# Low parts of the split weights 32 bytes off the other tiles, and the products of gate and up grouped by high and low

## The chip, the cores and the metric

The kernel runs on one core of a Trainium2 chip. The metric is the device time of one execution in microseconds, as the median of several runs. The names of the engines in the rows are PE (TensorE, the matmuls), PEld (its weight loads, which run beside the matmuls), DVE (VectorE), ACT (ScalarE), POOL (GpSimd) and SP (SyncE, which issues most of the DMAs).

## The reference

Two layers of a decoder trunk on 256 tokens of width 1024, all in float32. Each layer is a half-step SwiGLU network, a mixer of three kinds of attention heads with one input and one output projection, and a second SwiGLU network. The change touches the SwiGLU networks and the tiles in which all weights are split:

```python
def swiglu(h, w_gate, w_up, w_down):
    return (jax.nn.silu(h @ w_gate) * (h @ w_up)) @ w_down

for l in range(DEPTH):                                   # 2
    x = x + 0.5 * swiglu(rmsnorm(x, ffn1_norm[l]), ffn1_w_gate[l], ffn1_w_up[l], ffn1_w_down[l])
    h = rmsnorm(x, mix_norm[l])
    ...
    x = x + o @ w_out[l]
    x = x + 0.5 * swiglu(rmsnorm(x, ffn2_norm[l]), ffn2_w_gate[l], ffn2_w_up[l], ffn2_w_down[l])
return rmsnorm(x, final_norm)
```

w_gate and w_up are 1024 x 2816, w_down is 2816 x 1024.

## The kernel before

Every product of two float32 matrices is made of three products of a shorter format, fp32r: each operand is split into a high part (a copy rounded to fp32r) and a low part (what is left), and high x high, high x low and low x high are summed in PSUM. For a weight tile `raw` that has come by DMA, `split` (L91) makes the high part `wh` on ACT (L96) and the low part `wl` on DVE (L97). `split_tiles` (L77) takes both from rings of five buffers of 4096 bytes per partition. In the built program every one of these buffers, and every other tile of that size, begins at a multiple of 512 bytes within its partition. The normed input of a network is `xhl` (L180): for each of eight blocks k of 128 rows the 256 columns of the high part, then the 256 of the low part.

A network (`ffn`, L243) goes through 22 blocks f of 128 columns of gate and up. For f = 1 to 21 each of gate (bank `pg`, tag g0) and up (bank `pu`, tag g1) takes eight wide products, `wh` against high and low part of the input side by side (512 columns), and eight narrow ones, `wl` against the high part alone (256 columns); the list `steps` (L294 to L297) sets their order, and the loop at L299 issues them at L308. For f = 0 the list is another one (L282 to L292), of 256-column products alone. Behind the products of block f stand the twelve 512-column matmuls of `down` for block f - 1 (L251, by `mm3` and `mm` at L89): h hi x wh, h hi x wl in the rows' names `wl,hh`, and h lo x wh.

Between them lies the chain that makes h from the two banks: the second half of gate's bank copied out (ACT, L324), added to the first (DVE, L325), times the norm's row (L326), Silu (ACT, L327); the second half of up's bank copied (ACT, L330), added (DVE, L331), multiplied with the gate (L333), and h split (ACT `hh` L336, DVE `hl` L337). After the last block `take` (L263) adds the four sums into x_tok, and `norm_in` (L195) transposes it for what comes next. The mixer's projections use the same `wh` and `wl`.

The program's text is written stage by stage; the order in which each engine gets its instructions is set by a scheduler that builds the queues of all engines from the program, so a change in one engine's list can move instructions on the others. Each engine then runs its queue in order and waits on semaphores. All weight loads go over SP's queue in order, and a load waits for its `raw` buffer (ring of four) to be free.

At the start ACT's queue loads the small tables `norm_rows` (L119) and `pos_rows` (L137), which `late_columns` (L166) transposes on PE in block f = 1 of the first network; `compressed` in the mixer loads its `w2` (L647, L648).

A few tiles of before do not begin at a multiple of 512 bytes: `maskc`, which is streamed through PE in the mixer, begins 32 bytes off a multiple of 64 and 480 off one of 512, and `pcm`, which is loaded as the stationary operand of a transpose, 32 bytes off a multiple of 64 and 352 off one of 512. Neither is fp32r: `maskc` is bf16, `pcm` float32.

Of the kernel before, what the change touches and what calls it, by code (L numbers as in the profile page):

```python
# [10 lines left out]
F32 = mybir.dt.float32  # L11
# [8 lines left out]
T = 256  # L20
# [3 lines left out]
KD = D // 128  # L24
# [38 lines left out]
def trunk(ctx, tc, a, out):  # L63
# [4 lines left out]
    sb = ctx.enter_context(tc.tile_pool(name="sb", bufs=1))  # L68
    con = ctx.enter_context(tc.tile_pool(name="con", bufs=1))
    small = ctx.enter_context(tc.tile_pool(name="small", bufs=1))  # L70
    big.tile([128, 96], F32, name="pad")
    ps = ctx.enter_context(tc.tile_pool(name="ps", bufs=2, space=PSUM))

    def raw_tile():
        return sb.tile([128, 2048], F32, name="raw", tag="raw", bufs=4)

    def split_tiles(n):  # L77
        h = sb.tile([128, 1024], F32R, name="wh", tag="wh", bufs=5)
        lo = sb.tile([128, 1024], F32R, name="wl", tag="wl", bufs=5)
        return h[:, :n], lo[:, :n]  # L80

    def bank(tag):
        return ps.tile([128, 512], F32, name="bk" + tag, tag=tag, bufs=2)
# [32 lines left out]
    x_tok = big.tile([128, 2, D], F32, name="x_tok")  # L116
    for t in range(2):
        nc.sync.dma_start(x_tok[:, t], a["x"][0, t * 128:(t + 1) * 128, :])
    norm_rows = con.tile([64, 128], F32, name="norm_rows")  # L119
    r0 = 0  # L120
    gcol = {}
    first_rows = con.tile([16, 128], F32, name="first_rows")
# [11 lines left out]
    cosn, sinn = tab[:, :, 0:16], tab[:, :, 16:32]  # L134
    cosm, sinm = tab[:, :, 32:64], tab[:, :, 64:96]
    cmask, cvalid = tab[:, :, 96:111], tab[:, :, 111:112]
    pos_rows = con.tile([64, 128], F32, name="pos_rows")  # L137
    for i, n in enumerate(("nsa_cmp_pos_k", "nsa_cmp_pos_v")):
        nc.scalar.dma_start(pos_rows[32 * i:32 * i + 32], a[n].rearrange("l (j q) d -> (l j) (q d)", q=2))
    gbias = con.tile([128, DEPTH, 18], F32, name="gbias")  # L140
# [39 lines left out]
    xhl = big.tile([128, KD, 2, T], F32R, name="xhl")  # L180
    xh, xl = xhl[:, :, 0], xhl[:, :, 1]
    oh = big.tile([128, KD, T], F32R, name="oh")
    ol = big.tile([128, KD, T], F32R, name="ol")

    state = {}

    def late_loads():
        if state.pop("late", None):
# [44 lines left out]
    def mm3(o, w, mov, first, last):  # L233
        mm(o, w[0], mov[0], first, False)
        mm(o, w[0], mov[1], False, False)
        mm(o, w[1], mov[0], False, last)

    def load_unit(w, c, n):
        t = raw_tile().rearrange("p (k f) -> p k f", k=KD)[:, :, :n]
        nc.sync.dma_start(t, w[:, c:c + n].rearrange("(k p) f -> p k f", p=128))  # L240
        return t

    def ffn(pre, l, nxt=None, final=False, first=False):  # L243


        wg, wu, wd = a[pre + "_w_gate"][l], a[pre + "_w_up"][l], a[pre + "_w_down"][l]
        rb = None
        acc = {}
        hs, ds = {}, {}

        def down(f, t, c):  # L251
            h, lo = hs[f]
            w = (ds[f][0][:, c * 512:c * 512 + 512], ds[f][1][:, c * 512:c * 512 + 512])
            s = slice(t * 128, t * 128 + 128)
            mm3(acc[t, c], (h[:, s], lo[:, s]), w, f == 0, f == NF - 1)

        tokens_first = [(t, c) for t in range(2) for c in range(2)]
        columns_first = [(t, c) for c in range(2) for t in range(2)]
        order = tokens_first if final else columns_first

        def take(t, c):
            x = x_tok[:, t, c * 512:c * 512 + 512]
            DVE.scalar_tensor_tensor(x, acc[t, c], r05[:, t:t + 1], x, op0=OP.mult, op1=OP.add)  # L263

        for f in range(NF):
            o = 0
            if f % 2 == 0 or first and f == 1:
                n = 128 if first and f < 2 else 256
                if not (first and f == 0):
                    rg, ru = [load_unit(w, f * 128, n) for w in (wg, wu)]  # L270
            else:
                o = 128
            if f % 2 == 0:
                rd = raw_tile().rearrange("p (j f) -> p j f", j=2)
                nc.sync.dma_start(rd, wd[f * 128:f * 128 + 256, :].rearrange("(j p) f -> p j f", p=128))
            if first and f == 0:
                G, U = W0
            else:
                G = split(rg[:, :, o:o + 128], 1024, "p (k f) -> p k f", k=KD)
                U = split(ru[:, :, o:o + 128], 1024, "p (k f) -> p k f", k=KD)  # L280
            pg, pu = bank("g0"), bank("g1")
            if f == 0:  # L282
                if first:
                    groups = [(o, w, (k,)) for o, w in ((pg, G), (pu, U)) for k in (0, 2, 4, 6, 1, 3, 5, 7)]
                else:
                    groups = [(o, w, ks) for ks in ((0, 1, 2, 3), (4, 5, 6, 7)) for o, w in ((pg, G), (pu, U))]
                steps = []
                for o, w, ks in groups:
                    hi = [(o[:, :T], w[0], xh, k) for k in ks]
                    mid = [(o[:, :T], w[1], xh, k) for k in ks]  # L290
                    lo = [(o[:, T:], w[0], xl, k) for k in ks]
                    steps += hi + lo + mid if first else hi + mid + lo  # L292
            else:
                steps = []  # L294
                for o, w in ((pg, G), (pu, U)):
                    steps += [(o, w[0], xhl.rearrange("p k i q -> p k (i q)"), k) for k in range(KD)]
                    steps += [(o[:, :T], w[1], xh, k) for k in range(KD)]  # L297
            seen = {id(pg): 0, id(pu): 0}
            for j, (o, w, m, k) in enumerate(steps):  # L299
                b = id(pg) if o.tensor is pg.tensor else id(pu)  # L300
                last = not any(s[0].tensor is o.tensor for s in steps[j + 1:])
                args = (o, w[:, k], m[:, k])
                flags = dict(start=seen[b] == 0, stop=last, skip_group_check=True)
                seen[b] = 1
                if first and f == 0:
                    then("pe", PE.matmul, *args, **flags)
                else:
                    PE.matmul(*args, **flags)  # L308
            if f == 1:
                if state.get("late"):  # L310
                    late_columns()
                for i, (t, c) in enumerate(order):
                    acc[t, c] = bank("a%d" % (i // 2))
            if f > 0:
                for t, c in order if f < NF - 1 else order[:2]:
                    down(f - 1, t, c)
            if rb is None:
                r = rstd_col()
                r05 = small.tile([128, 2], F32, name="r05", tag="r05", bufs=2)
                DVE.tensor_scalar(r05, r, 0.5, None, op0=OP.mult)  # L320
                rb = rstd_rows(r)
            gn = tmp(0)[:, :T]
            g2 = tmp(3)[:, :T]
            ACT.copy(g2, pg[:, T:])  # L324
            DVE.tensor_tensor(gn, pg[:, :T], g2, op=OP.add)  # L325
            DVE.tensor_tensor(gn, gn, rb, op=OP.mult)  # L326
            ACT.activation(gn, gn, AF.Silu)  # L327
            un = tmp(1)[:, :T]
            u2 = tmp(3)[:, :T]
            ACT.copy(u2, pu[:, T:])  # L330
            DVE.tensor_tensor(un, pu[:, :T], u2, op=OP.add)  # L331
            h = tmp(2)[:, :T]
            DVE.tensor_tensor(h, gn, un, op=OP.mult)  # L333
            hh = sb.tile([128, T], F32R, name="hh", tag="hh", bufs=2)
            hl = sb.tile([128, T], F32R, name="hl", tag="hl", bufs=2)
            ACT.activation(hh, h, AF.Copy)  # L336
            DVE.tensor_tensor(hl, h, hh.bitcast(F32), op=OP.subtract)  # L337
            hs[f] = (hh, hl)
            ds[f] = split(rd[:, f % 2], 1024)
            if final and f == 2:  # L340
                state["fnorm"] = sb.tile([128, D], F32, name="fnorm", tag="pj")
                nc.sync.dma_start(state["fnorm"], a["final_norm"].partition_broadcast(128))
            if f == 3:
                late_loads()

        if final:
            for t in range(2):
                if t == 1:
                    for c in range(2):
                        down(NF - 2, t, c)  # L350
                sm = small.tile([128, 2], F32, name="fs", tag="fs", bufs=2)
                zs = []
                for c in range(2):
                    down(NF - 1, t, c)
                    take(t, c)
                    zs.append(finish(t, c, sm))
                store(t, zs, sm)
        else:
            for t in range(2):
                down(NF - 1, t, 0)  # L360
                take(t, 0)
            for t in range(2):
                down(NF - 2, t, 1)
            norm_in(nxt[0], nxt[1], 0)
            for t in range(2):
                down(NF - 1, t, 1)
                take(t, 1)
            norm_in(nxt[0], nxt[1], 1)
# [688 lines left out]
```

## Time and profile before

| | |
|---|---|
| median of three runs | 1042.52 us (1041.95 to 1046.9) |
| profiled execution, own time | 1044.06 us |
| its span in the trace | 1042.3 us |
| mean granted PE clock over the span (share of 2.4 GHz) | 0.997 |
| PE busy | 98% of the span |
| DVE, ACT busy | 67%, 56% |

The span is what the trace covers, from the first to the last instruction; the own time of the same execution is 1.8 us longer. In a timeline row the duration of a run of matmuls reaches from the first one's start to the modelled end of the last one; how fast PE goes is read from the distance between starts.

### The profile page before, as it was taken

What the parts mean: (1) busy time and instruction counts of PE and PEld (TensorE: products, weight loads), DVE (VectorE), ACT (ScalarE), POOL (GpSimd) and SP (SyncE); (2) the same over time, 40 slices, a digit from 0 to 9 for tenths busy, and PEclk for the clock granted to TensorE, in tenths of its full rate; (3) what the DMA queues carried; (4) which work ended last, traced back from release to release, by engine and by line L of the source; (5) the groups of instructions that cost most, each with busy time, mean ns of one, the idle gap of its engine ahead of it and who ended that gap; (6) DMA issues with size and microseconds to landing.
All of it is one profiled execution on the core that took longest, in us unless ns stands there. A gap on an engine that the chain in (4) does not pass through costs nothing.

```text
span 1042.3 us, 15114 instructions
## 1 busy us (share of the span) xinstructions
PE 1019.9 (98%) x5743; PEld 867.1 (83%) x5743; DVE 699.4 (67%) x1132; ACT 578.6 (56%) x1082; POOL 78.9 (8%) x137
## 2 busy tenths in 40 slices
PE   7999999999999999999999999999999999999996
PEld 6888888897877888888888888889868788888885
DVE  6666666766656766666676666667756577666664
ACT  5555555646666655555565555556456665555553
POOL 2000000033410000000000000002143000000001
PEclk9999999999999999999999999999999999999999
DMA  9555463572242646455445546465523344645531
GB/s 322 175 207 191 172 223 134 163 255 70 84 134 81 231 141 234 160 203 196 168 160 204 195 169 224 143 201 176 192 61 122 121 133 159 234 166 197 196 128 41
DMA packets 128404, 176.38 MB, mean 169 GB/s; under 512 B 4566, under 2 KB 107212, under 8 KB 128332
## 3 DMA queue, kind: packets, MB, share of 16 engines
q1 hardware_dynamic: 127840, 174.83, 49.5%
q8 instruction: 45, 0.74, 0.3%
q10 hardware_dynamic: 492, 0.59, 0.2%
q14 instruction: 27, 0.22, 0.1%
HBM read 174.36 MB, written 1.05 MB: 168 GB/s over the span
## 4 chain that ended last, share of the span: by engine, by line
PE 93%; DVE 3%; ACT 2%; issue 1%; DMA 1%; POOL 0%; POOLq 0%; SPq 0%; DVEq 0%; ACTq 0%
PE bkg L308 46%; PE bka L89 37%; PE bkg L89 6%; DVE wl L97 1%; PE bkg L632 1%; PE bkg L202 1%; ACT junk L213 0%; ACT wh L96 0%; DMA x_tok<-in_x_dram 0%; DMA raw<-in_ffn_w_up_dram 0%; ACT xhl L207 0%; PE bkg L782 0%; PE bkg L106 0%; DVE x_tok L263 0%; POOL wl L1018 0%
## 5 line engine op out<-in xcount | busy, mean ns | idle before, releaser
L97 DVE TENSOR_TENSOR wl<-raw,wh 128x1024 fp32r<-128x1024 f32 (+5 forms) x336 | 395.3, 1180 | 203.0 <-ACT wh L96 196.7
L96 ACT ACTIVATE wh<-raw 128x1024 fp32r<-128x1024 f32 (+5 forms) x336 | 340.4, 1016 | 232.0 <-PE bkg L308 175.8
L308 PE MATMUL bkg<-xhl,wh 128*128 128x512 f32 (+1 forms) x1440 | 349.0, 384 | 0.2 <-DVE xhl L208 0.2
L308 PEld LDWEIGHTS bkg<-xhl,wh 128*128 128x128 f32 x1440 | 259.5, 189 | 48.0 <-PE bkg L202 0.3
L308 PEld LDWEIGHTS bkg<-xhl,wl 128*128 128x128 f32 x1392 | 189.9, 190 | 13.1
L308 PE MATMUL bkg<-xhl,wl 128*128 128x256 f32 x1392 | 195.3, 282 | 0.0
L89 PE MATMUL bka<-wh,hh 128*128 128x512 f32 x352 | 139.4, 396 | 1.2 <-ACT hh L336 1.1
L89 PE MATMUL bka<-wl,hh 128*128 128x512 f32 x352 | 139.0, 395 | 0.0
L89 PE MATMUL bka<-wh,hl 128*128 128x512 f32 x352 | 137.4, 392 | 0.6 <-DVE hl L337 0.6
L336 ACT ACTIVATE hh<-t 128x256 fp32r<-128x256 f32 x88 | 36.8, 418 | 127.2 <-DVE t L333 127.2
L89 PE MATMUL bka<-wh,xhl 128*128 128x384 f32 (+4 forms) x384 | 106.8, 349 | 0.0
L89 PEld LDWEIGHTS bka<-wh,hl 128*128 128x128 f32 x352 | 66.6, 189 | 16.0 <-DVE hl L337 1.7
L89 PEld LDWEIGHTS bka<-wh,hh 128*128 128x128 f32 x352 | 66.7, 190 | 14.2 <-ACT hh L336 3.0
L89 PEld LDWEIGHTS bka<-wl,hh 128*128 128x128 f32 x352 | 66.7, 190 | 10.4
L89 PEld LDWEIGHTS bka<-wh,xhl 128*128 128x128 f32 x384 | 68.9, 188 | 5.7 <-issue 1.7
L89 PE MATMUL bka<-wl,xhl 128*128 128x384 f32 (+4 forms) x192 | 65.9, 343 | 0.0
L337 DVE TENSOR_TENSOR hl<-t,hh 128x256 fp32r<-128x256 f32 x88 | 37.4, 425 | 40.7 <-ACT hh L336 40.7
L222 POOL TENSOR_TENSOR r<-r,nhalf 128x2 f32<-128x2 f32 x5 | 3.5, 703 | 599.3 <-DVE r L221 599.3
L325 DVE TENSOR_TENSOR t<-bkg,t 128x256 f32<-128x256 f32 x88 | 36.8, 418 | 6.4 <-ACT t L324 6.4
L333 DVE TENSOR_TENSOR t<-t,t 128x256 f32<-128x256 f32 x88 | 37.4, 425 | 4.1 <-ACT t L327 1.3
L326 DVE TENSOR_TENSOR t<-t,rb 128x256 f32<-128x256 f32 x88 | 37.4, 425 | 2.8
L459 ACT ACTIVATE P<-bka,st 128x256 f32<-128x256 f32 (+1 forms) x72 | 29.4, 418 | 16.6 <-DVE st L763 11.3
(229 smaller groups left out, 933.2 us busy)
## 6 DMA issues: line engine op xcount, KB each, us to landing
raw<-in_ffn_w_down_dram SPq DMA_DIRECT2D x44, 1024.0 KB, 6.7
raw<-in_ffn_w_gate_dram SPq DMA_DIRECT2D x43, 1024.0 KB, 6.8
raw<-in_ffn_w_up_dram SPq DMA_DIRECT2D x43, 1024.0 KB, 5.2
raw<-in_w_in_dram SPq DMA_DIRECT2D x8, 768.0 KB, 4.6
raw<-in_w_out_dram SPq DMA_DIRECT2D x20, 256.0 KB, 3.6
raw<-in_w_in_dram SPq DMA_DIRECT2D x4, 1024.0 KB, 7.0
raw<-in_w_in_dram SPq DMA_DIRECT2D x4, 832.0 KB, 4.5
raw<-in_w_in_dram SPq DMA_DIRECT2D x4, 804.0 KB, 4.4
```

Of the source, the lines that this page charges most:

```text
L89: PE.matmul(o, l, r, start=start, stop=stop, skip_group_check=True)
L96: ACT.activation(hv, src, AF.Copy)
L97: DVE.tensor_tensor(lv, src, hv.bitcast(F32), op=OP.subtract)
L202: PE.transpose(p[:, i * T + t * 128:i * T + t * 128 + 128], x_tok[:, t, d * 128:d * 128 + 128], ident)
L308: PE.matmul(*args, **flags)
L325: DVE.tensor_tensor(gn, pg[:, :T], g2, op=OP.add)
L326: DVE.tensor_tensor(gn, gn, rb, op=OP.mult)
L333: DVE.tensor_tensor(h, gn, un, op=OP.mult)
L336: ACT.activation(hh, h, AF.Copy)
L337: DVE.tensor_tensor(hl, h, hh.bitcast(F32), op=OP.subtract)
L459: state["last_exp"] = ACT.activation(*args, **kw).ins
L632: PE.transpose(p[:96, s * T + t * 128:s * T + t * 128 + 128], src[t][:, 2 * pr + s], ident)
```

## The change

Two edits, and what the first needs. The ring of `wl` buffers now begins 32 bytes behind a multiple of 512 (a tile of 32 bytes is placed ahead of it, one of 480 bytes behind it), so that all other tiles stay where they stood by that measure: in the built program the first `wl` buffer moves from byte 115200 to 116256. To make room, `norm_rows` and `pos_rows` no longer have buffers of their own but use those of `hr` and `w2` of the mixer. And in the blocks f = 1 to 21 the order of the products is no longer gate high, gate low, up high, up low, but gate high, up high, gate low, up low.

```diff
     def split_tiles(n):
         h = sb.tile([128, 1024], F32R, name="wh", tag="wh", bufs=5)
+        if "pad" not in state:
+            state["pad"] = sb.tile([128, 8], F32, name="pad1", tag="pad1")
         lo = sb.tile([128, 1024], F32R, name="wl", tag="wl", bufs=5)
+        if state["pad"] is not None:
+            state["pad"] = sb.tile([128, 120], F32, name="pad2", tag="pad2") and None
         return h[:, :n], lo[:, :n]
...
-    norm_rows = con.tile([64, 128], F32, name="norm_rows")
+    norm_rows = sb.tile([128, 128], F32, name="norm_rows", tag="hr")[:64]
...
-    pos_rows = con.tile([64, 128], F32, name="pos_rows")
+    pos_rows = sb.tile([128, 128], F32, name="pos_rows", tag="w2")[:64]
...
             else:
                 steps = []
-                for o, w in ((pg, G), (pu, U)):
-                    steps += [(o, w[0], xhl.rearrange("p k i q -> p k (i q)"), k) for k in range(KD)]
-                    steps += [(o[:, :T], w[1], xh, k) for k in range(KD)]
+                for i, m in ((0, xhl.rearrange("p k i q -> p k (i q)")), (1, xh)):
+                    for o, w in ((pg, G), (pu, U)):
+                        steps += [(o if i == 0 else o[:, :T], w[i], m, k) for k in range(KD)]
```

On PE one block of the first network stood before as follows (bkg_369 is the gate's bank, bkg_370 the up's, bka the banks of the down sums):

```order
L308 MATMUL bkg_369<-xhl,wh 128x512 x8
L308 MATMUL bkg_369<-xhl,wl 128x256 x8
L308 MATMUL bkg_370<-xhl,wh 128x512 x8
L308 MATMUL bkg_370<-xhl,wl 128x256 x8
L89 MATMUL bka_319<-wh,hh 128x512
L89 MATMUL bka_319<-wl,hh 128x512
```

and stands now (lines have moved by four to six, the gate's bank is bkg_371, the up's bkg_372):

```order
L312 MATMUL bkg_371<-xhl,wh 128x512 x8
L312 MATMUL bkg_372<-xhl,wh 128x512 x8
L312 MATMUL bkg_371<-xhl,wl 128x256 x8
L312 MATMUL bkg_372<-xhl,wl 128x256 x8
L95 MATMUL bka_321<-wh,hh 128x512
L95 MATMUL bka_321<-wl,hh 128x512
```

The up's wide run has moved ahead of the gate's narrow run; nothing else in the block has moved on PE.

On DVE, at the end of the first network (block f = 21, then the four takes into x_tok; the 768-column splits are weights of the mixer), there stood before:

```order
L97 TENSOR_TENSOR wl<-raw,wh 128x768 x2
L325 TENSOR_TENSOR t_1872<-bkg_1832,t_1873 128x256
L326 TENSOR_TENSOR t_1872<-t_1872,rb 128x256
L97 TENSOR_TENSOR wl<-raw,wh 128x768
L331 TENSOR_TENSOR t_1878<-bkg_1833,t_1879 128x256
L333 TENSOR_TENSOR t_1882<-t_1872,t_1878 128x256
L337 TENSOR_TENSOR hl<-t_1882,hh 128x256
L263 SCALAR_TENSOR_TENSOR x_tok<-bka_319,r_240,x_tok 128x512
L263 SCALAR_TENSOR_TENSOR x_tok<-bka_320,r_240,x_tok 128x512
L263 SCALAR_TENSOR_TENSOR x_tok<-bka_321,r_240,x_tok 128x512
L97 TENSOR_TENSOR wl<-raw,wh 128x768
```

and stand now:

```order
L329 TENSOR_TENSOR t_1874<-bkg_1834,t_1875 128x256
L103 TENSOR_TENSOR wl<-raw,wh 128x768
L330 TENSOR_TENSOR t_1874<-t_1874,rb 128x256
L335 TENSOR_TENSOR t_1880<-bkg_1835,t_1881 128x256
L337 TENSOR_TENSOR t_1884<-t_1874,t_1880 128x256
L341 TENSOR_TENSOR hl<-t_1884,hh 128x256
L103 TENSOR_TENSOR wl<-raw,wh 128x768
L267 SCALAR_TENSOR_TENSOR x_tok<-bka_321,r_242,x_tok 128x512
L267 SCALAR_TENSOR_TENSOR x_tok<-bka_322,r_242,x_tok 128x512
L267 SCALAR_TENSOR_TENSOR x_tok<-bka_323,r_242,x_tok 128x512
L267 SCALAR_TENSOR_TENSOR x_tok<-bka_324,r_242,x_tok 128x512
```

The split that stood between the gate's product with the norm's row and the up's sum now stands one place earlier in the chain, and one more split stands between h's low part and the four takes.

On SP, at the start of the program, there stood before (L240 are the loads of gate and up, L275 those of down, w_2165 is the mixer's w2):

```order
L191 DMA gbias<-in_nsa_gate_bias_dram 128x36
L647 DMA w_2165<-in_nsa_cmp_w_k_dram 128x64
L240 DMA raw<-in_ffn_w_up_dram 128x8x128
L240 DMA raw<-in_ffn_w_gate_dram 128x8x256
L648 DMA w_2165<-in_nsa_cmp_w_v_dram 128x64
L240 DMA raw<-in_ffn_w_up_dram 128x8x256
```

and stand now:

```order
L195 DMA gbias<-in_nsa_gate_bias_dram 128x36
L244 DMA raw<-in_ffn_w_up_dram 128x8x128
L244 DMA raw<-in_ffn_w_gate_dram 128x8x256
L244 DMA raw<-in_ffn_w_up_dram 128x8x256
L279 DMA raw<-in_ffn_w_down_dram 128x2x1024
L244 DMA raw<-in_ffn_w_gate_dram 128x8x256
L651 DMA w_2167<-in_nsa_cmp_w_k_dram 128x64
L652 DMA w_2167<-in_nsa_cmp_w_v_dram 128x64
```

The two small loads of w2, which share a buffer with `pos_rows` now, have moved behind the loads of blocks 2 and 3 and the gate load of blocks 4 and 5.

## Rows read from the trace of the kernel before

**Rows 1.** Head of the page: the span, busy time by engine.

```profile
span 1042.3 us, 15114 instructions
...
PE 1019.9 (98%) x5743; PEld 867.1 (83%) x5743; DVE 699.4 (67%) x1132; ACT 578.6 (56%) x1082; POOL 78.9 (8%) x137
```

**Rows 2.** The page's chain that ended last, by engine.

```profile
PE 93%; DVE 3%; ACT 2%; issue 1%; DMA 1%; POOL 0%; POOLq 0%; SPq 0%; DVEq 0%; ACTq 0%
```

**Rows 3.** Timeline of PE, one block f of the first network: start, duration.

```profile
70.33 1.98 PE L308 MATMUL bkg<-xhl,wh 128*128 128x512 f32 x8
72.15 1.11 PE L308 MATMUL bkg<-xhl,wl 128*128 128x256 f32 x8
73.10 2.00 PE L308 MATMUL bkg<-xhl,wh 128*128 128x512 f32 x8
74.94 1.11 PE L308 MATMUL bkg<-xhl,wl 128*128 128x256 f32 x8
75.89 0.40 PE L89 MATMUL bka<-wh,hh 128*128 128x512 f32 x1
76.13 0.40 PE L89 MATMUL bka<-wl,hh 128*128 128x512 f32 x1
...
77.06 0.39 PE L89 MATMUL bka<-wh,hl 128*128 128x512 f32 x1
...
78.64 0.62 PE L308 MATMUL bkg<-xhl,wh 128*128 128x512 f32 x2
```

**Rows 4.** Windows: the same block; the granted clock follows POOL's column.

```profile
70.30:78.60 8.30, 8.30 (x45) 7.16 (x44) 5.62 (x8) 4.43 (x8) 0.00 (x0) 1.00 0.51 185
```

**Rows 5.** Groups by line, shapes apart: count, busy us, mean ns of one.

```profile
L308 PE MATMUL bkg<-xhl,wl 128*128 128x256 f32 x1392 | 195.3, 282 | 0.0
L89 PE MATMUL bka<-wl,hh 128*128 128x512 f32 x352 | 139.0, 395 | 0.0
```

**Rows 6.** Timeline of PE around one streamed `maskc`; then weight loads of `pcm` and `x_tok`.

```profile
237.10 0.39 PE L89 MATMUL bka<-maskc,identb 128*128 128x256 bf16 x2
...
L734 PEld LDWEIGHTS bkg<-ident,pcm 128*128 128x128 f32 x4 | 0.6, 140 | 1.5 <-PE bka L89 1.5
...
L202 PEld LDWEIGHTS bkg<-ident,x_tok 128*128 128x128 f32 x80 | 9.4, 140 | 5.3 <-DVE x_tok L263 2.0 <-DVE x_tok L952 1.8
```

**Rows 7.** Timeline of PE in block f = 0 of the first network, its last narrow products.

```profile
13.79 0.40 PE L106 MATMUL bkg<-xhl,wh 128*128 128x256 f32 x2
...
16.31 2.00 PE L308 MATMUL bkg<-xhl,wh 128*128 128x512 f32 x8
```

**Rows 8.** Timeline at the end of the first network: PE, then ACT, then DVE.

```profile
192.19 0.40 PE L89 MATMUL bka<-wh,hh 128*128 128x512 f32 x1
...
194.89 0.50 PE L89 MATMUL bka<-wh,hh 128*128 128x512 f32 x1
...
194.42 0.42 ACT L336 ACTIVATE hh<-t 128x256 fp32r<-128x256 f32 x1 [1.56 <-DVE t L333]
...
192.64 0.96 DVE L97 TENSOR_TENSOR wl<-raw,wh 128x768 fp32r<-128x768 f32 x1 [1.22 <-ACT wh L96]
194.87 0.43 DVE L337 TENSOR_TENSOR hl<-t,hh 128x256 fp32r<-128x256 f32 x1 [0.48 <-ACT hh L336]
195.91 1.44 DVE L263 SCALAR_TENSOR_TENSOR x_tok<-bka,r,x_tok 128x512 f32<-128x512 f32 x2 [0.61 <-PE bka L89]
```

**Rows 9.** Timeline at the start of the program, block f = 1: SP, ACT and PE.

```profile
10.14 0.44 SPq L647 DMA_DIRECT2D w<-in_nsa_cmp_w_k_dram  x1
10.69 0.38 SPq L240 DMA_DIRECT2D raw<-in_ffn_w_up_dram  x1
...
17.12 2.01 ACT L96 ACTIVATE wh<-raw 128x1024 fp32r<-128x1024 f32 x2 [1.87 <-DMA raw<-in_ffn_w_up_dram]
...
19.10 2.00 PE L308 MATMUL bkg<-xhl,wh 128*128 128x512 f32 x8
23.44 0.50 PE L89 MATMUL bka<-wh,hh 128*128 128x512 f32 x1 [1.12 <-ACT hh L336]
```

More of the change, by code (lines that the diff above doesn't have):

```diff
@@ L72, in trunk @@
     ps = ctx.enter_context(tc.tile_pool(name="ps", bufs=2, space=PSUM))
+    state = {}
     def raw_tile():
@@ L183, in trunk @@
     ol = big.tile([128, KD, T], F32R, name="ol")
-    state = {}
     def late_loads():
```

## The prediction

> **What bounds the kernel now.** I read the head of the page first: PE is busy 98% of a span of 1042.3 us [rows 1]. Then the chain of work that ended last: 93% of it is PE itself, and all other engines and the DMAs together hold 7% [rows 2]. So the time is the sum of the distances between PE's matmuls, and a change is worth what it takes from these distances, or the PE waits that it makes. The third view is the timeline of one block f [rows 3]: it has no wait in it, the next block begins 8.31 us after this one (78.64 - 70.33), and the granted clock there is 1.00, the upper level of 2.4 GHz [rows 4]. 84 such blocks (4 networks, f = 1 to 21) are 698 us, two thirds of the time.
>
> Inside the block the distances are these. A wide run behind another wide matmul takes 1.82 us for eight (72.15 - 70.33), 0.227 each; seven down matmuls take 1.58 (78.64 - 77.06), 0.226 each. A narrow run takes 0.95 (73.10 - 72.15, and 75.89 - 74.94), 0.119 each [rows 3]. At 2.4 GHz 512 columns are 213 ns and 256 are 107, so each matmul takes about 13 ns over its columns, wide or narrow.
>
> **Edit 1, the order of the products.** What can change is what happens where the width changes. The wide run behind a narrow one takes 1.84 us, 0.02 more than the one behind a wide matmul. The twelve down matmuls behind a narrow run take 2.75 (78.64 - 75.89) where 12 x 0.227 are 2.72: 0.03 more, and 0.24 for the first of them instead of 0.227 [rows 3]. A change from narrow to wide so costs 0.02 to 0.03 us. Before there are two in a block, afterwards one: 84 x 0.025 = 2.1 us come off. Something is given back: eight narrow products take 0.95, but in a long row of them each takes 0.120 (block 0: 21 products from 13.79 to 16.31, 2.52 us [rows 7]), which is 0.96 for eight, so the first ones of a narrow run are up to 0.01 cheaper, and there is one such start less in each block: 84 x 0.01 = 0.8 at most, of which I take 0.5. Edit 1 is worth **-1.6 us**, between -2.5 (84 x 0.03) and -0.8 (84 x 0.02, less 0.8). The same rows of block 0 answer the question whether sixteen narrow products in one run starve PE of weights: 48 in one run, with as many weight loads, go at 0.120 each.
>
> **Edit 1, its covers.** The up's high products need `wh` of up 1.8 us earlier than before, and the gate's bank is complete 1.8 us later, 0.95 ahead of the up's. In a steady block DVE is busy 5.62 and ACT 4.43 of 8.30 us [rows 4], the splits run a block ahead, and h of block f is wanted only behind the 5.5 us of products of block f + 1, so both are covered there. The cover ends at two places.
>
> The start: in block f = 1 the up's `wh` is split from 17.12 on, two splits of 1.0 us, ready at 18.13; the up's wide run starts at 19.10 now and would start at 16.31 + 1.82 = 18.13 [rows 7, 9]. That is just in time, and the up's load, issued at 10.69 behind the load of w2 at 10.14, moves up by as much as 0.55 us, since w2's loads go back in SP's queue [rows 9]. What is lost there, 0.5 at most, would go into the 1.12 us that PE waits for `hh` at 23.44 [rows 9]. I take **0** (-0.2 to +0.3). The later w2 loads are first needed in the mixer, some 180 us after.
>
> The ends of the networks: after f = 21 PE has only about a dozen down matmuls to run until it needs `hh`. At the first network's end the products end at 192.19 and `hh` lets PE go on at 194.89 [rows 8]. With the new order the gate's bank is complete at 192.19 - 0.95 = 191.24. From there: copy, sum, the 768-column split that now stands next on DVE (0.96), the product with the row, Silu, h, `hh`: six steps of about 0.42 and the split are 3.5 us, `hh` at 194.7 and with the hops between engines up to 195.2. That is -0.2 to +0.3 against now. Then one more split of 0.96 stands between h's low part and the takes, which start at 195.91 now [rows 8]; `hl` ends then at about 195.5, the split at 196.4: the takes come 0.5 later, part of it hidden by down matmuls and transposes. I take +0.5 for each of the two ends before a mixer (0 to +1.2), 0 for the end between the layers and the last one (each -0.5 to +0.5), together **+1.0 us**, between -0.5 and +2.9.
>
> **Edit 2, the 32 bytes.** It adds no instruction. It changes where PE's weight loads of 1392 narrow products and 352 down products read [rows 5], and where 352 of them stream from (down's weights are the streamed operand). No fp32r tile lies so in the kernel before, so I bound it from both sides. Nearest above and below zero are the two tiles that do lie 32 bytes off a multiple of 64. `maskc` is streamed: two of its 256-column matmuls take 0.39 us, and a pair of 256-column products of `wh`, which lies at a multiple of 512, takes 0.40 [rows 6, 7]. `pcm` is loaded as weights in 140 ns, as `x_tok` at a multiple of 512 is [rows 6]. Both say nothing is gained or lost, and I take **0**; both are other number formats, which is why the ends stay in the range. Upward the most that a distance in the block exceeds its like is 0.01 (0.24 against 0.227): 1744 x 0.01 = +17 us. Downward there is the 13 ns that each matmul takes over its columns: all of it off 1744 products would be -23, half of it -11.6 us.
>
> A rule bears on this: the Trainium skill, "TensorE: Matmul & The Clock Gate", section "Back-to-back issue gap", gives the isolated distance as columns / 2.4 + 2.5 ns, 109 ns for 256 columns, and says that in a real stream the weight load sets the distance too. The trace has 0.119, so something here costs 10 ns more than that figure; if the offset took it away from the narrow products, an estimate by the page is 1392 x 10 = -14 us, which would give 1028; its chance lies in that of the first rival below. Against any effect speaks "SBUF — State Buffer", section "Who interferes with whom", by which PE has read ports of its own.
>
> **The sum.** 1042.3 - 1.6 + 0 + 1.0 + 0 = 1041.7 us of span, -0.6. The profiled execution's own time of 1044.06 would become 1043.5. It stands 1.5 above the median of the runs shown, so against that median of 1042.52 I forecast **1041.9 us**. No change can be told by a measurement of this kernel below about 0.5%, 5.2 us.
>
> **The rivals.**
>
> *The offset frees PE* (faster). The stationary operand is loaded while the other streams, and today both begin at a multiple of 512; if the 13 ns come from the two meeting, moving one frees them. For it: all fp32r matmuls show the same 13 ns, whatever their width, so it isn't the columns. Against it: `maskc`'s pair and `pcm`'s loads show nothing, and `wh`, which stays, shows the same 13 ns. At half of it on 1744 products: 1041.9 - 11.6 = 1030; on the gate's and up's narrow ones alone (1392 x 6.5 = 9): 1033. Chance 0.25.
>
> *The offset costs PE* (slower). If a row of 128 weights that begins 32 bytes late takes one more step to read, each load of `wl` is longer, and the narrow products, whose 0.119 us are shorter than a load (`pcm`'s 0.140 [rows 6]), can't hide it. From 5.2 / 1392 = 3.7 ns a product on, it decides: at 6 ns 1042 + 8 = 1050, at the bound 1059. Against it: `pcm`'s 140 ns. Chance 0.11.
>
> *The chain is the new bound* (a wait for the one removed). The later gate bank and the splits ahead of h make PE wait at all four ends and at the start at their dear values: +2.9 + 0.8 + 0.3 - 0.8 = +3.2, 1045.7. For it: the order on DVE at the first network's end. Chance 0.09.
>
> **How the numbers follow.** The forecast case, within 0.5%, has 0.55, the dear ends 0.09, which are within 0.5% as well; with the small half of the offset's cases either way that is 0.63 for no change. Faster by over 0.5%: 0.26, the freeing offset and a little of the tail. Slower: 0.11. The likeliest case alone lies between 1039.5 and 1045. The range reaches down to 1030 so as to hold most of the freeing offset, and up to 1047; outside stay the costly offset (0.09 or so) and a gain over 12 us (0.06).
>
> **What would show it.** Right, if in the profile after: a block begins 8.29 us after the last; the up's wide run takes 1.82 behind the gate's, and the sixteen narrow products about 1.91; weight loads and distances of `wl` products are as before; `hh` at the first network's end comes between 194.5 and 195.3 if all before it is moved by the same. Wrong, if narrow products stand at other than 0.119 to 0.120 or the down matmuls with `wl` differ from their neighbours (offset), or if PE waits inside a block or over 1.5 us more at the ends (chain).

## The result, and the profile after

The changed kernel takes 1050.97 us in the median of its runs, beside 1043.28 us for the kernel before; the ratio is 1.0066, with a 95% interval from 1.0052 to 1.0079. It is slower by some 6.9 us, outside the range of the prediction. Its profiled execution took 1049.2 us.

The head of the page and the chain that ended last, to compare with [rows 1, 2]:

```profile
span 1047.4 us, 15075 instructions
...
PE 1022.1 (98%) x5743; PEld 864.2 (83%) x5743; DVE 671.0 (64%) x1132; ACT 587.7 (56%) x1082; POOL 79.0 (8%) x137
...
PE 91%; DVE 4%; ACT 3%; DMA 1%; issue 1%; POOL 0%; POOLq 0%; DVEq 0%; ACTq 0%
```

PE still fills 98% of the span. Its share of the chain has gone from 93% to 91%, but that is a share of one path traced back and not a loss: the time in which PE is not busy has gone from 22.4 us (1042.3 - 1019.9) to 25.3 (1047.4 - 1022.1). The 5.1 us between the two spans are not yet the 6.9 us of the medians: the profiled execution of before held a stretch at the lower clock level near the start, which that of after did not. In the windows of that stretch, of before,

```profile
25.30:28.70 3.40, 3.40 (x9) 2.62 (x9) 2.20 (x4) 1.90 (x6) 0.00 (x0) 0.50 0.61 218
```

and of after,

```profile
25.30:28.70 3.40, 3.40 (x16) 2.77 (x15) 3.21 (x6) 2.63 (x5) 0.00 (x0) 1.00 0.68 229
```

the granted clock (behind POOL's column) is 0.50 and 1.00, its lower and its upper level (1.2 and 2.4 GHz), which is 3.4 x 0.5 = 1.7 us in after's favour.

The chain of work in the second network, pieces of PE in order of time (start, length, count):

```profile
399.99 2.79 PE bka L95 x12
402.77 5.57 PE bkg L312 x32
408.34 2.79 PE bka L95 x12
```

A block is 8.35 us from start to start (408.34 - 399.99), where it was 8.31 [rows 3]; forecast was 8.29. The twelve down matmuls take 2.79 instead of 2.75, and the 32 products of gate and up 5.57, where the old order had 5.56. The timeline of one down run shows how:

```profile
72.29 2.05 PE L312 MATMUL bkg<-xhl,wl 128*128 128x256 f32 x16
74.18 0.40 PE L95 MATMUL bka<-wh,hh 128*128 128x512 f32 x1
...
75.10 0.40 PE L95 MATMUL bka<-wl,hh 128*128 128x512 f32 x1
...
76.97 3.38 PE L312 MATMUL bkg<-xhl,wh 128*128 128x512 f32 x14
```

Before, the distances were a little long for some five matmuls behind a narrow run and then settled at 0.226 [rows 3: from 77.06 on]. Now the last eight take 76.97 - 75.10 = 1.87, 0.234 each: they don't settle. The sixteen narrow products take 1.89 (74.18 - 72.29), 0.118 each; they are not slower but a trifle faster.

The second place is between the networks of the two layers. Windows of both kernels, the blocks 1 to 21 of the second network (from the first product of block 1 to that of block 21) and the stretch from there to block 1 of the third; of before:

```profile
344.40:510.70 166.30, 166.30 (x884) 143.50 (x883) 114.39 (x164) 90.12 (x145) 0.00 (x0) 1.00 0.55 192
510.70:531.80 21.10, 19.55 (x122) 16.68 (x121) 15.03 (x26) 13.58 (x28) 0.70 (x1) 1.00 0.52 175
```

and of after:

```profile
344.10:511.20 167.10, 167.10 (x882) 142.99 (x881) 107.21 (x164) 91.97 (x144) 0.00 (x0) 1.00 0.58 189
511.20:534.40 23.20, 19.76 (x124) 16.88 (x122) 14.90 (x27) 13.65 (x28) 0.69 (x1) 1.00 0.50 172
```

The blocks have no wait in them in either kernel (PE's busy time is the whole window), so their 0.8 us are distances. The stretch between the networks is 2.1 us longer with PE's busy time nearly the same: there it is waits. PE's idle time in it has gone from 1.55 us (21.10 - 19.55) to 3.44 (23.20 - 19.76). The timeline of before, PE, then ACT, then DVE:

```profile
524.83 0.88 PE L202 MATMUL bkg<-ident,x_tok 128*128 128x128 f32 x6 [1.00 <-DVE x_tok L263]
...
518.63 0.42 ACT L336 ACTIVATE hh<-t 128x256 fp32r<-128x256 f32 x1 [1.52 <-DVE t L333]
519.19 1.06 ACT L96 ACTIVATE wh<-raw 128x1024 fp32r<-128x1024 f32 x1
...
518.17 0.43 DVE L333 TENSOR_TENSOR t<-t,t 128x256 f32<-128x256 f32 x1
```

The timeline of after, in the same order:

```profile
519.33 0.40 PE L95 MATMUL bka<-wh,hl 128*128 128x512 f32 x1
521.17 0.50 PE L95 MATMUL bka<-wh,hh 128*128 128x512 f32 x1 [1.45 <-ACT hh L340]
525.88 0.88 PE L206 MATMUL bkg<-ident,x_tok 128*128 128x128 f32 x6 [0.22 <-DVE x_tok L267]
528.41 0.86 PE L312 MATMUL bkg<-xhl,wh 128*128 128x256 f32 x5 [1.65 <-DVE xhl L212]
...
519.76 1.06 ACT L102 ACTIVATE wh<-raw 128x1024 fp32r<-128x1024 f32 x1 [1.00 <-PE bka L95]
520.72 0.40 ACT L340 ACTIVATE hh<-t 128x256 fp32r<-128x256 f32 x1
...
519.36 0.42 DVE L337 TENSOR_TENSOR t<-t,t 128x256 f32<-128x256 f32 x1
520.85 1.23 DVE L103 TENSOR_TENSOR wl<-raw,wh 128x1024 fp32r<-128x1024 f32 x1 [1.07 <-ACT wh L102]
523.10 2.73 DVE L267 SCALAR_TENSOR_TENSOR x_tok<-bka,r,x_tok 128x512 f32<-128x512 f32 x4 [0.69 <-PE bka L95]
```

Before, `hh` came as soon as h was ready, at 518.60, and the split `wh` behind it. Now h is ready on DVE at 519.78, but on ACT a weight split stands ahead of `hh`: it waits for a buffer that PE's down matmuls give free, runs to 520.82, and only then comes `hh`. PE waits 1.45 us for it. The takes then run four in a row, the norm comes late, and PE waits another 1.65. From the start of the block's products, h is 0.66 us later than before (519.78 - 511.20 = 8.58, before 518.60 - 510.68 = 7.92) and `hh` 1.57 (9.52 and 7.95): the larger part of its delay is the split on ACT, the rest lies ahead of h.

### The profile page after: what moved, and what is told of

It is laid out like the page before. It is cut to its first block, busy times and chain, and to the rows that moved or that the text cites. A ratio compares the mean times of both kernels' runs of the same rounds, so it can differ in the third digit from the quotient of the medians.

```text
span 1047.4 us, 15075 instructions
## 1 busy us (share of the span) xinstructions
PE 1022.1 (98%) x5743; PEld 864.2 (83%) x5743; DVE 671.0 (64%) x1132; ACT 587.7 (56%) x1082; POOL 79.0 (8%) x137
## 4 chain that ended last, share of the span: by engine, by line
PE 91%; DVE 4%; ACT 3%; DMA 1%; issue 1%; POOL 0%; POOLq 0%; DVEq 0%; ACTq 0%
PE bkg L312 46%; PE bka L95 37%; PE bkg L95 6%; DVE wl L103 1%; ACT wh L102 1%; DMA raw<-in_ffn_w_gate_dram 1%; PE bkg L636 1%; PE bkg L206 0%; DMA x_tok<-in_x_dram 0%; ACT xhl L211 0%; ACT junk L217 0%; PE bkg L786 0%; DVE x_tok L267 0%; POOL wl L1022 0%; PE bka L112 0%
## 5 line engine op out<-in xcount | busy, mean ns | idle before, releaser
L312 PE MATMUL bkg<-xhl,wh 128*128 128x512 f32 (+1 forms) x1440 | 337.1, 385 | 1.9 <-DVE xhl L212 1.6
L312 PEld LDWEIGHTS bkg<-xhl,wh 128*128 128x128 f32 x1440 | 264.4, 188 | 58.9 <-DVE xhl L212 1.9
L312 PEld LDWEIGHTS bkg<-xhl,wl 128*128 128x128 f32 x1392 | 177.3, 188 | 7.2
L312 PE MATMUL bkg<-xhl,wl 128*128 128x256 f32 x1392 | 180.2, 281 | 0.0
L331 ACT ACTIVATE t<-t 128x256 f32<-128x256 f32 x88 | 36.7, 418 | 78.8 <-DVE t L330 78.7
L334 ACT COPY t<-bkg 128x256 f32<-128x256 f32 x88 | 32.8, 372 | 45.4 <-PE bkg L312 45.3
```

## The experiments

All are compared by a block's length, which the profiled execution of each gives twenty times over: the first wide product of the second network's last block, less that of its block 1, over 20. It was 8.313 before ((510.68 - 344.43) / 20) and is 8.357 after ((511.20 - 344.06) / 20).

### Each edit alone

The new order alone (a1_order), which is the last hunk of the diff on the kernel before:

> The new order of gate and up alone, all tiles at multiples of 512 bytes as before. Theory (the 32 bytes make the change slow, where the low weights are streamed or loaded): a block takes 8.28 to 8.29 us, the down run 2.75 behind the narrow run, and the time is within 2 us of before (ratio 0.998 to 1.002). Rival (the order itself is slow, by its long narrow run or by the ends of the networks): the blocks take 8.35 us or the ends cost as in the changed kernel, ratio 1.004 or more.

```profile
402.23 5.54 PE bkg L308 x32
407.77 2.75 PE bka L89 x12
410.52 5.54 PE bkg L308 x32
```

The chain of work shows the block at 8.29 (410.52 - 402.23; over twenty 8.293), exactly 0.02 below before. The time was 1044.1 us beside 1042.81, ratio 1.0014 (in brackets here and below the 95% interval: 1.0005 to 1.0023): the blocks are better and the kernel still a little slower. The first theory holds for the blocks, the rival for the ends; the windows show where:

```profile
343.90:509.80 165.90, 165.90 (x884) 143.57 (x882) 107.11 (x164) 91.94 (x144) 0.00 (x0) 1.00 0.57 190
509.80:534.40 24.60, 21.14 (x123) 18.37 (x122) 14.90 (x27) 13.62 (x28) 0.69 (x1) 0.93 0.47 163
...
526.90:531.00 4.10, 4.06 (x21) 4.06 (x22) 2.27 (x7) 1.93 (x6) 0.69 (x1) 0.58 0.81 256
```

The stretch between the networks takes 24.6 us instead of 21.1: the same two waits of 1.45 and 1.65 us as in the changed kernel, and in this execution a fall of the granted clock behind the second wait (a mean of 0.58 from 526.9 to 531).

The 32 bytes alone (a2_offset), which is the diff without its last hunk:

> The low weights 32 bytes off alone, products in the old order. Theory (the 32 bytes): a block takes 8.35 us or more, down runs 2.78, ratio 1.004 to 1.008. Rival (the order): blocks as before at 8.31, ratio within 0.998 to 1.002.

```profile
401.70 2.80 PE bka L95 x12
404.50 5.58 PE bkg L312 x32
```

1049.71 us, ratio 1.0063 (1.0049 to 1.0077); the stretch between the networks is as before (513.28 to 534.45, 21.2 us), the down run is 2.80 (2.75 before), and the block 8.385 in the second network and 8.365 in the third ((701.75 - 534.45) / 20). So the offset alone makes nearly the whole loss: with the old order it costs a block 0.05 to 0.07, with the new one 0.064 (8.357 - 8.293).

### Which operand the offset hurts

`wl` is the loaded operand in gate and up and the streamed one in down. In the changed kernel the low weights that down streams are taken from a multiple of 512 again (a3_down_al); z is the column, of 4 bytes, at which the slice for each half c of the output begins:

```diff
-            w = (ds[f][0][:, c * 512:c * 512 + 512], ds[f][1][:, c * 512:c * 512 + 512])
+            z = (120, 504)[c]
+            w = (ds[f][0][:, c * 512:c * 512 + 512], ds[f][1][:, z:z + 512])
```

> The changed kernel, but down streams its low weights from addresses 480 bytes further on, at a multiple of 512 (columns shifted, so the sums differ; the same number of operations). Gate's and up's low weights are still loaded from 32 bytes off. If the streamed operand is what the offset hurts: down runs fall from 2.78 to 2.75, the sixteen wide products from 3.68 to 3.63, the block to 8.27 to 8.29, ratio to before 0.998 to 1.003. If the loaded operand is: the blocks stay at 8.35 and the ratio at 1.005 or more.

```profile
401.72 5.53 PE bkg L313 x32
407.25 2.77 PE bka L95 x12
410.02 5.53 PE bkg L313 x32
```

The block is 8.299 ((509.38 - 343.39) / 20), 0.006 above the new order alone, and the ratio 1.0031 (1.0019 to 1.0044). Both lie just outside what was expected for the streamed operand, and far from the 8.35 for the loaded one. The reverse, on the kernel before with the new order and `z = (8, 392)[c]` (a4_down_off):

> All tiles at multiples of 512 bytes, the new order, but down streams its low weights from 32 bytes past a multiple of 512 (columns shifted, so the sums differ). If the streamed operand is what the offset hurts: down runs 2.78, sixteen wide products 3.68, block 8.35 to 8.37, ratio 1.004 to 1.007. If the loaded operand is: block 8.28 to 8.29, ratio within 0.998 to 1.002.

```profile
399.89 2.77 PE bka L89 x12
402.66 5.57 PE bkg L309 x32
408.23 2.77 PE bka L89 x12
```

Block 8.345 ((510.92 - 344.02) / 20), ratio 1.0056 (1.0043 to 1.0068). Here no tile has moved, so neither the writes of the splits nor the new places of the small tables play a part. So of the 0.064 us 0.052 (a4_down_off) to 0.058 (8.357 - 8.299, a3_down_al) come from four streams a block in down, and the offset of the loaded operand is worth next to nothing: its 0.006 are the difference of a narrow run that is 0.02 shorter and of the last wide matmul ahead of it and the down matmuls behind it, which are 0.026 longer together. Half of the 0.052 falls in the down run itself (2.77 for 2.75), half in the wide run that follows (5.57 for 5.54), which streams from where it always did: what the offset stream starts lasts some matmuls beyond it.

### Which offsets, and how many streams

The same kernel as a4_down_off, with 64 bytes (`z = (16, 400)[c]`), 256 bytes (`(64, 448)`), 128 (`(32, 416)`) and 480 (`(120, 504)`):

> As the run in which only down streams its low weights from 32 bytes off (block 8.345 us against 8.293 with the new order alone), but 64 bytes off. Theory (a stream of 2048 bytes that begins 32 past a multiple of 64 touches one piece of 64 bytes more): block back to 8.293, down run 2.748. Rival (any difference to the other tiles' place by 512 costs): block 8.34 to 8.35.

> The same with 256 bytes. Theory of pieces of 64 bytes: block 8.293. Rival (place by 512): 8.33 to 8.35. If 64 bytes cost and 256 don't, or the other way, the size of the piece lies between them.

> New order, tiles as before, down streams its low weights from 128 bytes off (columns shifted, so the sums differ). With 64 bytes the block is 8.340, with 256 it is 8.293. If what counts is the place within 256 bytes: 8.33 to 8.35. If it is the place within 128: 8.293.

> The same with 480 bytes, 32 short of a multiple of 512. If any place off the multiple costs alike: 8.33 to 8.36. If only the first bytes behind a multiple cost: 8.293.

Each of the four is a single execution; in all four the block of the third and of the fourth network has the same length as that of the second, to 0.001 us.

| offset of down's `wl` | block, us | more than at 0 |
|---|---|---|
| 0 | 8.293 | |
| 32 bytes | 8.345 | 0.052 |
| 64 bytes | 8.340 | 0.047 |
| 128 bytes | 8.326 | 0.033 |
| 256 bytes | 8.293 | 0.000 |
| 480 bytes | 8.378 | 0.085 |

The chain of work with 256 bytes is that of the new order alone:

```profile
401.25 5.54 PE bkg L309 x32
406.79 2.75 PE bka L89 x12
409.54 5.54 PE bkg L309 x32
```

With 480 bytes it is:

```profile
400.69 2.79 PE bka L89 x12
403.49 5.58 PE bkg L309 x32
```

The theory of pieces of 64 bytes has fallen, since 64 cost nearly as much as 32, and so has the one that any place off a multiple of 512 costs, since 256 is free. Of the places tried, those off a multiple of 256 bytes cost, but not alike: 128 is just below the 8.33 to 8.35 expected, 480 (32 short of 512) above its 8.33 to 8.36. Nor does the cost fall in the same place: at 64 bytes nearly all of it is in the down run itself (2.79, and 5.54 for the products behind it), at 32 and 480 the products pay a good part (5.57 and 5.58).

High and low weights of down both streamed from 32 bytes off (b3_both32, a single execution too), all twelve streams of a block:

> New order, tiles as before, but down streams high and low weights both from 32 bytes off (columns shifted, so the sums differ). Theory (each stream that begins 32 off costs by itself): 12 matmuls instead of 4 pay, block 8.29 + 3 x 0.052 = 8.40 to 8.45. Rival (the change between streams on and off the multiple costs): block 8.29 to 8.31.

```profile
402.64 2.80 PE bka L89 x12
405.45 5.57 PE bkg L309 x32
411.01 2.80 PE bka L89 x12
```

Block 8.372 ((514.05 - 346.61) / 20): 0.079 more than at 0, neither three times the 0.052 nor nothing, so neither expectation held. A down matmul takes 0.233 on the mean (2.80 / 12) where at 0 it takes 0.229 (2.75 / 12) and, once settled, 0.227. There is no fixed price for a stream off the multiple: four streams at 32 bytes cost 0.052, twelve 0.079, and four at 480 bytes 0.085.

### The ends, and a version that beats both

The new order in blocks 1 to 20, the old one in the last block of each network, no offset (b4_last_old):

```diff
+                if f < NF - 1:
+                    runs = [(i, o, w) for i in range(2) for o, w in ((pg, G), (pu, U))]
+                else:
+                    runs = [(i, o, w) for o, w in ((pg, G), (pu, U)) for i in range(2)]
...
```

> New order in blocks 1 to 20, the old one in the last block of each network, all tiles as before. If the loss of the order alone comes from the chain to h behind the last block: the stretch between the networks of the two layers falls from 24.6 us to 21.1 to 21.5, those around the mixers to 157.8, the blocks stay at 8.293, and the time is 1 to 2 us below before (ratio 0.998 to 0.9995). If not: ratio 1.001 or more, as with the new order throughout.

```profile
344.30:510.10 165.80, 165.80 (x882) 143.54 (x881) 107.05 (x164) 92.08 (x144) 0.00 (x0) 1.00 0.56 190
510.10:531.30 21.20, 19.65 (x124) 16.75 (x122) 15.25 (x27) 13.90 (x28) 0.70 (x1) 1.00 0.53 190
...
518.07 0.42 ACT L341 ACTIVATE hh<-t 128x256 fp32r<-128x256 f32 x1 [1.52 <-DVE t L338]
518.63 1.06 ACT L96 ACTIVATE wh<-raw 128x1024 fp32r<-128x1024 f32 x1
```

The windows show the better blocks with the old stretch between the networks, and ACT's rows show `hh` ahead of the split again. 1041.27 us beside 1042.94, ratio 0.9982 (0.9973 to 0.9991): faster than the kernel before by 1.9 us (0.9 to 2.8 by the interval), where 80 blocks at 0.02 give 1.6, and by the two ratios some 9 below the changed one.

The changed kernel with the same edit (c3_after_last):

> The changed kernel with the old order in the last block of each network alone. If its loss is the sum of the streamed offset and of the last blocks' order: the blocks stay at 8.357, the stretch between the layers' networks falls from 23.2 to 21.1 to 21.5, and the ratio to before is 1.003 to 1.005, between the changed kernel's 1.0066 and 1. If the ends have nothing to do with it: 1.006 or more.

```profile
343.30:510.50 167.20, 167.20 (x884) 143.08 (x883) 107.11 (x164) 92.18 (x144) 0.00 (x0) 1.00 0.57 189
510.50:531.60 21.10, 19.55 (x123) 16.63 (x122) 15.16 (x27) 13.86 (x28) 0.69 (x1) 1.00 0.54 187
```

1046.5 us beside 1042.4, ratio 1.0040 (1.0027 to 1.0054), with the blocks at 8.357 and the stretch at 21.1. The loss is the sum of the two. ACT's order and DVE's at the ends go back together in both runs, so the price of the one without the other is not measured.

## Why the prediction was wrong

**The step that failed** is the term of edit 2, "I take 0". The offset costs 80 blocks x 0.064 = 5.1 us against the new order alone, and 0.4 us in each of the two stretches around a mixer, which hold a network's last block and the mixer's projections, and these stream `wl` too (343.33 - 185.24 = 158.1 us with the offset and the old last block, 344.25 - 186.55 = 157.7 with that order and no offset).

I settled the term by two tiles of another format, `maskc` with 256 columns of bf16 and `pcm` as a loaded operand, and neither is the case that counts: 512 columns of fp32r, streamed. The pair of `maskc`, read to 0.01 us and to a modelled end, could hardly have shown 0.006 a matmul either. The upper bound, +17 us, held the loss, though it was counted over the wrong products: the 352 products of down with `wl` load `hh` and not `wl`, so they are streams and no loads, and the projections' streams of `wl` were left out.

Nor is it quite so that the kernel before had nothing of the kind: no fp32r tile begins off a multiple of 512 there, but slices do. In the mixer's input projection, products of 402 and 416 columns of `wh` and `wl` begin, in every second group, at byte 1608 or 1664 of the buffer, 72 or 128 past a multiple of 256. They stand 0.184 and 0.189 us apart in the median (three of 416 columns from 235.77 to 236.34), where products of 384 columns, which begin at a multiple, stand 0.173 apart and settle; at 2.4 GHz the 18 and 32 columns more would make 0.181 and 0.186 of it, by estimate. So the trace of before held a hint of 0.003 us a matmul; no run tells it from an effect of the number of columns.

The rival that the offset costs PE gave the right sign by the wrong mechanism: it put the loss on the loads of `wl` in gate and up, and there the runs show 0.006 us a block (a3_down_al); it is the streams of down. That its 1050 us are close to the 1050.97 measured is luck. The rule that I cited against any effect, the Trainium skill, "SBUF — State Buffer", "Who interferes with whom", does not carry that far: PE's ports may be its own, but the distance of its matmuls depends on where the streamed operand begins, by about 0.006 us of 0.227 where all twelve down streams are off (b3_both32).

**The ends**, taken as +1.0, came to +2.8. For the two ends ahead of the mixers +0.5 each was nearly right: `hh` came at 193.89, in a network whose last block began 1.07 us earlier than before (185.56 for 186.63), so 0.5 later than 194.42 [rows 8] within it, and the stretches are 0.4 us longer (343.93 - 185.72 = 158.2 with the new order alone, 157.8 before).

```profile
193.89 0.42 ACT L340 ACTIVATE hh<-t 128x256 fp32r<-128x256 f32 x1 [0.49 <-DVE t L337]
...
195.95 2.72 DVE L267 SCALAR_TENSOR_TENSOR x_tok<-bka,r,x_tok 128x512 f32<-128x512 f32 x4
```

That is in part luck, since two sizes in it were off: `hh` was forecast 0.2 earlier to 0.3 later, and the takes, forecast 0.5 later, come 1.1 later within the network (195.95 + 1.07 - 195.91), of which the matmuls hid more than half. For the end between the layers I took 0, and the runs show 2.0. There I followed DVE's order, which has no split between the takes any more, and not ACT's, where a split had moved ahead of `hh`. In the order of the built program this is to be seen beforehand: a split into `wh` ahead of `hh`, which has to wait until PE gives its buffer free.

**The order in the blocks** was right: forecast -1.6 us, measured 84 x (8.293 - 8.313) = -1.7, by one change from narrow to wide less in each block. So were the covers inside the blocks, where PE never waited, the start (0.28 us of wait for the up's `wh`, which the wait for `hh` behind it gave back, 0.77 us for 1.12), and that sixteen narrow products in one run are no trouble. Rows 7 show this for 21 products in a row, not for 48 as the prediction says; the conclusion holds all the same.

**The sum by measured terms**: in 80 blocks (the last of each network lies in the stretch behind it) -1.6 for the order and +5.1 for the offset, +0.8 for the offset in the stretches around the mixers, +2.0 and 2 x 0.4 for the order at the ends make +7.1, where the ratio says 6.9.

**What stays open** is why the place of a stream matters. The runs show that a start 256 bytes on is free and the other four tried are not, that the cost falls on the run with the offset stream and in part on the matmuls behind it, and that 32 bytes on the loaded operand of the narrow products cost next to nothing. That the place within 256 bytes alone decides is likely from this but not shown, since no two offsets with the same place in it were tried except 0 and 256. Whether streams meet the weight loads at some common place, or a stream off the multiple needs one more access, no run here tells; the cost at 128 bytes, smaller than at 32, and at 480, larger, fits no simple count that I know of. Offsets of the input `xhl` or of `hh` were not tried.

## What to carry to other kernels

A tile's place in memory can be a term of the sum even where it adds no instruction: try the offset by itself on the operand that is streamed, at the width that is used, before it is taken as free; here a slice that begins at another column did it in one line. When a step's order changes in a loop, its price is often paid where the loop ends, so look at what stands ahead of the chain there on every engine, not on the one alone that the change names. An order that is good inside a loop and bad at its end can be kept inside and left off in the last round.

## What the runs showed of the hardware

A 512-column fp32r matmul, once settled, takes 0.227 us from start to start when its stream begins at a multiple of 256 bytes in the partition (a1_order, b2_down256), and about 0.233 when it and its neighbours begin 32 bytes off it (the twelve down matmuls of b3_both32). A change from narrow to wide products costs about 0.027 us over five matmuls (medians over the blocks of the kernel before for the first wide ones: 0.233, 0.236, 0.228, 0.232, 0.231, where a settled one takes 0.227). The granted clock fell to its lower level, 1.2 GHz, in some executions behind waits of PE of 1 to 2 us, at the start of the kernel before (0.50 from 25.3 to 28.7, behind a wait of 1.12) and between the networks with the new order alone (a mean of 0.58 from 526.9 to 531, behind one of 1.65), and in others behind the same waits it did not (1.00 in the changed kernel's stretch between the networks). It cost 1.4 to 1.7 us a time (24.6 - 23.2, and 3.4 x 0.5), so two profiles of kernels that differ by less must be compared stretch by stretch.
